# Two more gate pairs as seven half products ahead of attention, and a quota on the filler inside it

## The chip, the cores and the metric

The kernel runs on one core of one Trainium2 chip. The metric is the device time of one execution in microseconds (us). Engines are named as in the profile: PE is the tensor engine's matrix multiply, PEld its weight load, DVE the vector engine, ACT the scalar engine, POOL the general engine, SP the engine that here only issues transfers.

## The reference

One step of a one-layer hybrid encoder, for a prompt of 1024 rows and a sample of 64 rows, all in float32 with 1024 channels:

```python
xn = rms_norm(x, g_pre)
z = xn @ w_in                      # 1024 x 8208
xa, ga, q, k, v, gb, fl, ma, mb = jnp.split(z, np.cumsum(sizes)[:-1], axis=-1)
ua, conv_new = causal_conv(xa, conv_hist, conv_w, conv_b)
ya, h_new = rg_lru(ua, h0, w_rg_a, b_rg_a, w_rg_x, b_rg_x, a_param)
ya = ya * jax.nn.silu(ga)
yb = fox_prompt(q, k, v, logf)     # 16 heads of 64, causal, with forget sums
yb = yb.reshape(B, L, W_B) * jax.nn.silu(gb)
u = jnp.einsum('bsnw,nwd->bsnd', jnp.stack([ya, yb], axis=2), w_branch)
gates = jax.nn.sigmoid(jnp.stack([ma, mb], axis=2))
mix = jnp.sum(gates * u, axis=2) @ w_o
h = x + rms_norm(mix, g_post)      # then a gated per-layer embedding is added
```

`ga`, `gb`, `ma` and `mb` are the four gates: 1024 columns of the input projection each. They need nothing but `xn`, and are wanted only long after attention.

## The kernel before, in words

**Numbers.** A float32 operand is held as a rounded high part and a low part. A product is three matmuls, high by high, high by low and low by high (`three`, L169, whose matmuls carry L170, L171 and L172). The 1088 rows of `xn` (prompt and sample) lie transposed in SBUF.

**Two ways to make 256 columns of the projection.** A *panel* is 128 output columns: for each of three chunks of rows (364, 364, 360) eight steps over the inner dimension, each of three matmuls (`panel_steps`, L189). So a panel is 24 steps or 72 matmuls, and a pair of panels 144. A *quad* makes 256 output columns at once: weights and input are cut into two by two blocks, and seven products of half size stand for eight (`seven`, L860; `product`, L799, whose matmuls carry L805). A quad is seven products of 24 matmuls of 272 rows, so 168 matmuls. It needs sums of weight blocks, made by POOL, ACT and DVE (`split_pair`, L641), and sums of the input blocks, made once.

**The stages in order.** Values (v) for all rows come first (0 to 128 us of the span), then two plain panels (128 to 152), then the quads (152 to 418): eight for k and q, two for some columns of branch A, and `MORE` pairs taken from the end of the list `gates` (L226, L233), here two pairs of `gb`. Results of gates are stored to DRAM. Then comes attention (about 437 to 860 us), then branch A, the two branch projections, the output projection and the tail.

**Attention and its filler.** For each of 16 heads there are four blocks of 256 queries, in the order 0, 3, 1, 2 (`units`, L1242; `q2` is the block's number). A block takes *scores* (matmuls L1125 and L1126; then on DVE the mask and maximum, L1105, on ACT the exponential, L1107, on DVE the reciprocal, L1109, on POOL the scaling, L1110), *turns* (transposes to PSUM, L1147; then ACT copies the high part `th` and DVE the low part `tl`; for the diagonal part the tiles are `diag0h`, `diag0l` and so on) and *values* (four matmuls a turn, L1175 and L1177; then ACT and DVE join the halves in `lo` and `y`). Eight small steps belong to the sample. The gate panels that are left are the *filler*: `filler` (L1038) yields after each step of three matmuls into `acc`. Each panel of filler also brings a weight split (`wh` on ACT, `wl` on DVE, booked by `book_split`, L1021) and three copies out of PSUM (`st` on ACT).

**What sets the order.** PE's order is fixed when the program is built, by a loop (L1333) that keeps a clock `now` of PE and books of ACT, DVE and POOL with costs written in the kernel. A step of scores, turns or values is taken if its inputs have been ready on that clock for `SLACK` = 600 ns. Otherwise a step of filler is taken, if there is one. If there is none, the clock jumps to the moment at which the first step gets ready. ACT, DVE and POOL work in the order of the same books. Before the change 17 panels, 408 steps, are filler.

Of the kernel before, what the change touches and what calls it, by code (L numbers as in the profile page):

```python
# [15 lines left out]
KT = D // P  # L16
# [16 lines left out]
CW = HT // 2  # L33
PLAIN = 2

MORE = 2
W_SC = 1092
GC = 364

# [4 lines left out]
D_W = 1240.0  # L44

AHEAD = 4000
WAKE = 36
GA_EARLY = (1, 3, 5)
LN1P = [1.0 / 15, 1.0 / 13, 1.0 / 11, 1.0 / 9, 1.0 / 7, 1.0 / 5, 1.0 / 3]
# [16 lines left out]
def hybrid_step(tc, a, o):  # L66
# [11 lines left out]
    def f(ap):  # L78
        return ap.bitcast(F32)

    def copy_act(out, in_, scale=1.0):
        return act.activation(out=out, in_=in_, func=AF.Copy, scale=scale)  # L82
# [140 lines left out]
    def cols(c, n=2):  # L223
        return w_in[:, c:c + n * P]

    gates = deque((cols(c + k * P), (d[k], d[k + 1])) for c, d in ((C_MA, d_ma), (C_MB, d_mb), (C_GB, d_gb))  # L226
                  for k in range(0, KT, 2))
# [3 lines left out]
    for (s1, d1), (s2, d2) in (some[:2], some[2:]):  # L231
        quads.append(([s1, s2], (("r", d1), ("r", d2))))
    for _ in range(MORE):  # L233
        src, (d1, d2) = gates.pop()
# [13 lines left out]
    ahead = deque()  # L248
# [8 lines left out]
    def look_ahead():  # L257

        while len(ahead) < 2:
            if held_back[0] and len(gates) <= n_gates - PLAIN // 2:  # L260
                return
            if not (gates or later):
                return
            src, tags = (gates or later)[0]
            if any(not e[3] and max(len(tags), e[4]) > 1 for e in ahead):
                return
            (gates or later).popleft()
            if len(tags) > 1:
                dst = raw_pair
                raws_ = panels(raw_pair)  # L270
            else:
                dst = raw_half[n_single[0] % 2].rearrange("p (k n) -> p k n", k=KT)
                raws_ = [dst]
                n_single[0] += 1
            load_panel(dst, src, tc.keep_in_program_order)
            for tag, raw in zip(tags, raws_):
                ahead.append([tag if isinstance(tag, tuple) else ("r", tag), raw, None, False, len(tags)])
# [26 lines left out]
    def spill(dst, t0, n, z, s=None):  # L304
        s = s or wpool.tile([P, GC], F32, name="st")
        copy_act(s[:, :n], z)
        act.dma_start(dst[:, t0:t0 + n], s[:, :n])
# [141 lines left out]
    g_p = mm.tile([P, 512], F32, name="g_p", tag="acc")  # L449
    for i in range(WAKE):  # L450
        if i == WAKE - 8:
            pe.transpose(g_p[:, :KT], g8[:, :], ident[:KT, :KT])
# [528 lines left out]
    def spent(ns):  # L981
        now[0] += ns

    def book(engine, at, ns, do=None):

        busy = booked[engine]
        while busy and busy[0][1] < now[0] - 20000.0:
            busy.pop(0)
        i = 0
        while i < len(busy) and busy[i][0] < at + ns:  # L990
            at = max(at, busy[i][1])
            i += 1
        busy.insert(i, (at, at + ns))
        if do is not None:
            serial[0] += 1
            heapq.heappush(agenda, (at, serial[0], do))
        return at + ns + HOP

    def catch_up(to=None):
        to = now[0] if to is None else to  # L1000
        while agenda and agenda[0][0] <= to:
            heapq.heappop(agenda)[2]()
# [18 lines left out]
    def book_split():  # L1021

        if ahead and ahead[0][2] is None:
            e = ahead[0]
            raw = e[1]
            wh = wpool.tile([P, KT, P], F32R, name="wh")
            wl = wpool.tile([P, KT, P], F32R, name="wl")
            e[2] = wh, wl

            def low():  # L1030
                sub(dve, wl[:, :, :], raw, f(wh[:, :, :]))
                e[3] = True
                look_ahead()

            at = book("A", now[0] + 5000.0, A_W, lambda: copy_act(wh[:, :, :], raw))
            book("D", at, D_W, low)

    def filler():  # L1038
        left = deque()
        nxt = first_fill  # L1040
        while True:
            if nxt is None:
                look_ahead()
                if not ahead or ahead[0][0][0] != "r":
                    return
                nxt = ahead.popleft()[:3:2]
            (_, dst), w = nxt
            nxt = None
            book_split()

            def evac(c, t0, n, z, dst=dst):
                def do():
                    spill(dst, t0, n, z)
                    left.popleft()

                left.append(book("A", now[0] + 497.0 + HOP_PE, A_ST, do))

            for _ in panel_steps(mm, *w, xs, evac):
                spent(497.0)
                if len(left) > 1:  # L1060
                    catch_up(left[0])
                yield True
# [21 lines left out]
    def load_sample(p):  # L1084
        cols = slice(p * P, (p + 1) * P)
        t = {n: p2.tile(s, F32, name=n, tag=n, bufs=1) for n, s in (("kc", [P, P]), ("vc", [P, P]), ("vn", [DEC, P]))}
        sp.dma_start(t["kc"][:, :], a["cache_k"][:, cols])
        sp.dma_start(t["vc"][:, :], a["cache_v"][:, cols])
        sp.dma_start(t["vn"][:, :], o["v_sample"][:, cols])
        sp.dma_start(f(cs_k[2:, :]), d_cs[2 * p:2 * p + 2].rearrange("h s t -> (h s) t"))  # L1090
        sp.dma_start(f(cs_q[:2, :]).rearrange("s (h t) -> s h t", h=2), d_cq[:, 2 * p:2 * p + 2, :])
        t["ks"] = [p2.tile([P, LS], F32R, name=f"ks{i}", tag=f"ks{i}", bufs=1) for i in "hl"]
        for i in range(2):
            sp.dma_start(f(t["ks"][i][:, PAST:]), d_k[i, p][:, SEQ:])
            for j in range(2):
                js = slice(j * HD, (j + 1) * HD)
                sp.dma_start(f(qs[i][js, js]), d_q[i, p][js, SEQ:])
        smp[p] = t
        smp_at[p] = now[0] + (12000.0 if p else 24000.0)
# [142 lines left out]
    units = [(h, q2) for h in range(NH) for q2 in (0, 3, 1, 2)]  # L1242
    U = len(units)
    UP = 8
    s_q, t_q, v_q = deque(), deque(), deque()
# [46 lines left out]
    def go(step):  # L1292
        kind, x, i = step
        if kind == "s":
            h, q2 = units[x]
            big = q2 >= 2
            tag = "pb" if big else "pm"
            pr = p2.tile([P, 1024 if big else 512], F32, name=tag, tag=tag, bufs=4)
            prs.setdefault(x, []).append(pr)
            s_free["s2" if big else "s1"], due[step] = scores(h, q2, i, pr)  # L1300
            if x == 1 and i == 0:
                load_head(1)
            elif x % 4 == 3 and i == 1:
                load_head(h + 2)
        elif kind == "ss":
            s_free["s1"], due[step] = sample_scores(x)
        elif kind == "v":
            values(x, i, *units[x])
            seen["v"] += 1
            if i == units[x][1] and x % UP in (3, 5) and x // UP + 1 < NP:  # L1310
                load_v(x // UP + 1, x % UP // 4)
        elif kind == "sv":
            sample_values(x)
            if x + 1 < NP:
                load_sample(x + 1)
        else:
            t_free.popleft()
            if kind == "t":
                due[step] = turn(x, i, units[x][1], prs[x])
                seen["t"] += 1  # L1320
            else:
                due[step] = (sample_keys if kind == "sk" else sample_turn)(x)
            t_free.append(due[step])
        done.add(step)
# [4 lines left out]
    load_v(0, 0)  # L1329
    load_v(0, 1, "pb")  # L1330
    load_sample(0)
    fill = filler()
    while s_q or t_q or v_q:  # L1333
        catch_up()
        times = [(i, ready(q[0])) for i, q in enumerate((s_q, t_q, v_q)) if q]
        times = [(i, at) for i, at in times if at is not None]
        best = next((i for i, at in times if at + SLACK <= now[0]), None)
        if best is None:
            if next(fill, False):
                continue  # L1340
            at, best = min((at, i) for i, at in times)
            now[0] = max(now[0], at)
            catch_up()
        go((s_q, t_q, v_q)[best].popleft())
    while next(fill, False):
        catch_up()
    catch_up(float("inf"))
# [266 lines left out]
    fill = panel_steps(mm, *w, xs, lambda c, t0, n, z: spill(d_mb[KT - 1], t0, n, z))  # L1614
# [62 lines left out]
    for of in range(KT):  # L1677
        g = g_next
# [287 lines left out]
    def turn_h(b, pl=None):  # L1966
# [6 lines left out]
        for g in range(3):  # L1973
# [7 lines left out]
            h, l = th[:, k_, :n], (tl[:, k_, :n] if n == P else th[:, k_, DEC:])  # L1981
            with tc.high_priority(AHEAD):
                copy_act(h, t)
# [166 lines left out]
    ss, r = tiny(n, "ss"), tiny(n, "r_r")  # L2150
# [55 lines left out]
```

## Time and profile before

| what | value |
|---|---|
| time, median of three runs | 1464.6 us (1464.26 to 1467.74) |
| the profiled execution's own time | 1467.15 us |
| its span, first to last instruction | 1465.4 us |
| PE busy | 1436.0 us (98%) |
| DVE busy | 893.7 us (61%) |
| ACT busy | 717.1 us (49%) |
| POOL busy | 299.1 us (20%) |
| mean granted clock of PE | 0.994 |

The profiled execution's own time lies 2.55 us above the median, and 1.75 us of its time lie outside its span. PE's matmuls overlap, so a matmul's duration in the profile (0.33 us for 364 rows) is longer than its share of PE's time, and the distance from one start to the next is what counts. A row of the view by windows gives for each engine the busy us and, in brackets, the number of instructions; "acc" are the matmuls of panels, "quad" those of quads.

### The profile page before, as it was taken

What the parts mean: (1) busy time and instruction counts of PE and PEld (TensorE: products, weight loads), DVE (VectorE), ACT (ScalarE), POOL (GpSimd) and SP (SyncE); (2) the same over time, 40 slices, a digit from 0 to 9 for tenths busy, and PEclk for the clock granted to TensorE, in tenths of its full rate; (3) what the DMA queues carried; (4) which work ended last, traced back from release to release, by engine and by line L of the source; (5) the groups of instructions that cost most, each with busy time, mean ns of one, the idle gap of its engine ahead of it and who ended that gap; (6) DMA issues with size and microseconds to landing.
All of it is one profiled execution on the core that took longest, in us unless ns stands there. A gap on an engine that the chain in (4) does not pass through costs nothing.

```text
span 1465.4 us, 25652 instructions
## 1 busy us (share of the span) xinstructions
PE 1436.0 (98%) x9653; PEld 1394.7 (95%) x9653; DVE 893.7 (61%) x1631; ACT 717.1 (49%) x1353; POOL 299.1 (20%) x385
## 2 busy tenths in 40 slices
PE   8999999999999999999999999999999999999997
PEld 8999999999999999999899989999999999879997
DVE  5464866564325666666466555898755574778534
ACT  4423444442215566666456556777444232554633
POOL 0013324323123332333233210221023000000001
PEclk9999999999999999999999999999999999999999
DMA  8457456754276565646545344454278774224111
GB/s 285 143 119 109 130 163 189 181 178 127 78 210 157 120 148 139 141 112 139 118 129 128 61 108 70 86 101 84 99 235 273 257 218 152 100 86 171 43 43 44
DMA packets 149304, 200.64 MB, mean 137 GB/s; under 512 B 24212, under 2 KB 115836, under 8 KB 148156
## 3 DMA queue, kind: packets, MB, share of 16 engines
q1 hardware_dynamic: 129772, 167.06, 44.2%
q10 hardware_dynamic: 17680, 25.64, 5.1%
q0 software_dynamic: 1728, 6.29, 2.3%
q8 instruction: 76, 1.25, 0.4%
q14 instruction: 48, 0.39, 0.1%
HBM read 131.04 MB, written 65.80 MB: 134 GB/s over the span
## 4 chain that ended last, share of the span: by engine, by line
PE 84%; DVE 7%; ACT 4%; DMA 3%; issue 2%; SPq 0%; POOL 0%; ACTq 0%; DVEq 0%; POOLq 0%
PE quad L805 17%; PE acc L170 12%; PE acc L172 12%; PE acc L171 12%; PE q L1853 5%; PE tp L1147 4%; PE pv L1175 2%; PE s L1125 2%; PE s L1126 2%; PE pv L1177 2%; PE vacc L170 1%; PE vacc L171 1%; PE vacc L172 1%; PE vacc L471 1%; PE q L1978 1%
## 5 line engine op out<-in xcount | busy, mean ns | idle before, releaser
L170 PE MATMUL acc<-xh,wh 128*128 128x364 f32 (+1 forms) x768 | 253.2, 330 | 1.3 <-ACT st L82 1.2
L171 PE MATMUL acc<-xl,wh 128*128 128x364 f32 (+1 forms) x768 | 252.0, 328 | 0.0
L172 PE MATMUL acc<-xh,wl 128*128 128x364 f32 (+1 forms) x768 | 251.8, 328 | 0.0
L170 PEld LDWEIGHTS acc<-xh,wh 128*128 128x128 f32 x768 | 144.9, 189 | 2.6 <-ACT st L82 1.9
L171 PEld LDWEIGHTS acc<-xl,wh 128*128 128x128 f32 x768 | 144.7, 188 | 0.5
L172 PEld LDWEIGHTS acc<-xh,wl 128*128 128x128 f32 x768 | 144.5, 188 | 0.0
L1105 DVE CUSTOM_DVE_ANT_0 s<-s,mask 128x1024 f32<-128x1024 f32 (+7 forms) x128 | 95.5, 767 | 26.8 <-PE s L1126 26.7
L85 DVE TENSOR_TENSOR wl<-w_raw,wh 128x1024 fp32r<-128x1024 f32 (+1 forms) x54 | 62.6, 1160 | 67.3 <-ACT wh L82 66.3
L1110 POOL TENSOR_SCALAR pb<-pb,sm 128x896 f32<-128x896 f32 (+1 forms) x64 | 61.8, 966 | 196.2 <-DVE sm L1109 178.2
L82 ACT ACTIVATE wh<-w_raw 128x1024 fp32r<-128x1024 f32 (+1 forms) x66 | 64.3, 976 | 65.6 <-PE quad L805 27.3
L85 DVE TENSOR_TENSOR tl<-tp,th 128x512 fp32r<-128x512 f32 x96 | 65.7, 688 | 35.6 <-ACT th L82 35.6
L805 PE MATMUL quad<-xh,wh 128*128 128x272 f32 x384 | 80.7, 291 | 0.0
L805 PE MATMUL quad<-xl,wh 128*128 128x272 f32 x384 | 79.5, 288 | 0.0
L805 PE MATMUL quad<-xh,wl 128*128 128x272 f32 x384 | 79.4, 288 | 0.0
L82 ACT ACTIVATE th<-tp 128x512 fp32r<-128x512 f32 x96 | 56.9, 596 | 40.6 <-PE tp L1147 33.4
L1107 ACT ACTIVATE pb<-s,nm 128x896 f32<-128x896 f32 (+1 forms) x64 | 61.1, 954 | 30.0 <-DVE nm L1105 27.7
L1125 PE MATMUL s<-k,q 128*128 128x256 f32 (+1 forms) x192 | 67.1, 353 | 0.2 <-ACT pb L1107 0.2
L1147 PE MATMUL tp<-ident,pb 128*128 128x128 f32 x416 | 63.9, 274 | 1.2 <-DVE diag0l L85 0.7
L1126 PE MATMUL s<-k,q 68*128 68x256 f32 (+1 forms) x192 | 65.0, 350 | 0.0
L171 PE MATMUL acc<-ybl,wh 128*128 128x364 f32 (+1 forms) x192 | 62.9, 328 | 0.0
L172 PE MATMUL acc<-ybh,wl 128*128 128x364 f32 (+1 forms) x192 | 62.8, 327 | 0.0
L170 PE MATMUL acc<-ybh,wh 128*128 128x364 f32 (+1 forms) x192 | 62.7, 326 | 0.0
(705 smaller groups left out, 4151.8 us busy)
## 6 DMA issues: line engine op xcount, KB each, us to landing
w_raw<-in_w_in SPq DMA_DIRECT2D x56, 256.0 KB
q<-d_q SPq DMA_DIRECT2D x48, 256.0 KB
k<-d_k SPq DMA_DIRECT2D x48, 256.0 KB
w_raw<-in_w_in SPq DMA_DIRECT2D x64, 128.0 KB
w_raw<-in_w_branch SPq DMA_DIRECT2D x32, 256.0 KB
wl<-w_raw POOLq DMA_DIRECT2D x12, 512.0 KB, 4.6
wraw<-in_w_in SPq DMA_DIRECT2D x20, 256.0 KB
d_k<-oh ACTq DMA_DIRECT2D x16, 272.0 KB
```

What stands on the lines that cost most here:

```text
L82: return act.activation(out=out, in_=in_, func=AF.Copy, scale=scale)
L85: return eng.tensor_tensor(out=out, in0=in0, in1=in1, op=ALU.subtract)
L170: pe.matmul(out, ah, bh, start=start, stop=False)
L171: pe.matmul(out, ah, bl, start=False, stop=False)
L172: pe.matmul(out, al, bh, start=False, stop=stop)
L805: pe.matmul(acc[:, c, :CW], l[:, k, :], r[:, k, c * CW:(c + 1) * CW], start=(first and k == 0 and p == 0), stop=(k == 3 and p == 2), skip_ ...
L1105: at = book("D", now[0] + HOP_PE, per(D_MAX, n), lambda: dve.tensor_tensor_reduce(out=s[:, :n], in0=s[:, :n], in1=m, scale=-1.0, scalar=-N ...
L1110: return free, book("G", at, per(G_NORM, n), lambda: pool.tensor_scalar(out=pr[:, :n], in0=pr[:, :n], scalar1=sm, scalar2=1.0, op0=ALU.mul ...
L1125: pe.matmul(s[:, c0:c0 + w], t["q1"][:, q0:q0 + P], t["k1"][:, c0:c0 + w], start=True, stop=False)
L1126: pe.matmul(s[:, c0:c0 + w], t["q2"][:HD + 4, q0:q0 + P], t["k2"][:HD + 4, c0:c0 + w], start=False, stop=True)
L1147: pe.transpose(tp[:, o0 + i * P:o0 + (i + 1) * P], pr[par][:, kb * P:(kb + 1) * P], ident[:, :])
L1853: pe.matmul(acc, l[:, k, :], r[:, k, :], start=(first and k == 0 and i == 0), stop=(k == 3 and i == 2), skip_group_check=not first)
```

## The change

`MORE` becomes 4: the pairs of `gb` columns 0 to 3 of eight leave the filler and become two more quads, so there are 14 quads and 13 panels, 312 steps, of filler. And the loop no longer takes filler whenever nothing else is ready. The first `HEAD` = 72 steps (three panels) are free; after that the number of steps taken may not run ahead of the share of attention's own PE work that is done, weighed by columns (`own_time`). If the quota is used up, the clock jumps to the next step's moment, as it did before when no filler was left.

```diff
-MORE = 2
+MORE = 4
...
+HEAD = 72
...
+    def own_time(step):
+
+        kind, x, i = step
+        if kind == "s":
+            full = 256 * (units[x][1] + 1)
+            return sum(2 * (0.44 * min(512, full - c0) + 8) for c0 in range(0, full, 512))
+        if kind == "t":
+            return 109.0 * (3 if i == units[x][1] else 4)
+        return {"v": 480.0, "sk": 109.0, "ss": 440.0, "st": 218.0, "sv": 840.0}[kind]
+
     fill = filler()
+    own_total = sum(own_time(step) for q in (s_q, t_q, v_q) for step in q)
+    own = 0.0
+    filled = 0
+    n_fill = 3 * KT * (1 + sum(e[0][0] == "r" for e in ahead) + sum(len(g[1]) for g in gates))
     while s_q or t_q or v_q:
...
         if best is None:
-            if next(fill, False):
+            if filled < HEAD + (n_fill - HEAD) * own / own_total and next(fill, False):
+                filled += 1
                 continue
             at, best = min((at, i) for i, at in times)
             now[0] = max(now[0], at)
             catch_up()
-        go((s_q, t_q, v_q)[best].popleft())
+        step = (s_q, t_q, v_q)[best].popleft()
+        own += own_time(step)
+        go(step)
```

The order on PE is the same up to the early heads and differs after them. The first place is in head 10, between the turn of its block 0 (three transposes into `tp`) and the values of that turn (`pv<-diag1l`). In both orders four values matmuls of another block and the first matmul of the sample's scores (`s<-ksh,qsh`) follow the turn; the rows below begin behind these. This is PE before:

```order
L170 MATMUL s_8620<-ksh,qsh 128x192
L171 MATMUL s_8620<-ksl,qsh 128x192
L172 MATMUL s_8620<-ksh,qsl 128x192
L1209 MATMUL s_8620<-cs_k,cs_q 128x192
L1147 MATMUL tp_8630<-ident,pb 128x128 x4
L170 MATMUL acc<-xh_110,wh 128x360
L171 MATMUL acc<-xl_112,wh 128x360
L172 MATMUL acc<-xh_110,wl 128x360
L170 MATMUL acc<-xh_110,wh 128x360
L171 MATMUL acc<-xl_112,wh 128x360
L172 MATMUL acc<-xh_110,wl 128x360
L1147 MATMUL tp_8650<-ident,pb 128x128 x4
```

The values `pv<-diag1l` stand in the row behind. The same place on PE with the change (lines are one higher):

```order
L171 MATMUL s_8832<-ksh,qsh 128x192
L172 MATMUL s_8832<-ksl,qsh 128x192
L173 MATMUL s_8832<-ksh,qsl 128x192
L1210 MATMUL s_8832<-cs_k,cs_q 128x192
L171 MATMUL acc<-xh_109,wh 128x364
L172 MATMUL acc<-xl_111,wh 128x364
L173 MATMUL acc<-xh_109,wl 128x364
L1176 MATMUL pv<-diag1l,vv 128x256
```

One step of filler and two turns of the next block have gone from between the turn and its values. The second place is the last block of the last head, where before no filler is left. PE before, three turns and the values of earlier ones:

```order
L1147 MATMUL tp_10525<-ident,pb 128x128 x4
L1175 MATMUL pv<-tl,vv 128x256
L1177 MATMUL pv<-th,vv 128x256
L1175 MATMUL pv<-tl,vv 128x256
L1177 MATMUL pv<-th,vv 128x256
L1147 MATMUL tp_10539<-ident,pb 128x128 x4
L1175 MATMUL pv<-diag2l,vv 128x256
L1177 MATMUL pv<-diag2h,vv 128x256
L1175 MATMUL pv<-diag2l,vv 128x256
L1177 MATMUL pv<-diag2h,vv 128x256
L1147 MATMUL tp_10554<-ident,pb 128x128 x3
```

The same turns with the change:

```order
L1148 MATMUL tp_10594<-ident,pb 128x128 x4
L1176 MATMUL pv<-tl,vv 128x256
L1178 MATMUL pv<-th,vv 128x256
L1176 MATMUL pv<-tl,vv 128x256
L1178 MATMUL pv<-th,vv 128x256
L171 MATMUL acc<-xh_110,wh 128x360
L172 MATMUL acc<-xl_112,wh 128x360
L173 MATMUL acc<-xh_110,wl 128x360
L1148 MATMUL tp_10612<-ident,pb 128x128 x4
L1176 MATMUL pv<-diag2l,vv 128x256
L1178 MATMUL pv<-diag2h,vv 128x256
```

A step of filler now stands between each turn and the next to the end of attention.

## The prediction, made before the changed kernel ran

> **What bounds the kernel now.** I read the page first, then the windows of the stages that the change touches, then PE's waits in attention, then single places in time. The page:
>
> ```profile
> span 1465.4 us, 25652 instructions
> PE 1436.0 (98%) x9653; PEld 1394.7 (95%) x9653; DVE 893.7 (61%) x1631; ACT 717.1 (49%) x1353; POOL 299.1 (20%) x385
> ...
> PE 84%; DVE 7%; ACT 4%; DMA 3%; issue 2%; SPq 0%; POOL 0%; ACTq 0%; DVEq 0%; POOLq 0%
> ```
>
> PE is busy for 98% of the span and is 84% of the chain that ended last: the kernel is bound by PE, and only what makes PE's work less, or makes PE wait, moves the time. By windows: the two plain panels, a stretch of quads that write gates, attention while filler lasts, its end without filler, and a stretch with a dip.
>
> ```profile
> 128.00:152.00 24.00, 23.91 (x145) 23.60 (x144) 18.95 (x16) 11.76 (x17) 11.40 (x8) 1.00 0.58 91
> 340.00:400.00 60.00, 60.00 (x480) 60.00 (x479) 24.33 (x33) 15.08 (x24) 11.82 (x8) 1.00 0.27 76
> 437.00:843.00 406.00, 402.32 (x2714) 387.08 (x2713) 250.86 (x649) 238.81 (x561) 132.08 (x198) 1.00 0.57 127
> 843.00:860.00 17.00, 13.61 (x95) 11.42 (x94) 10.52 (x24) 11.07 (x25) 3.92 (x8) 1.00 0.61 123
> 700.00:750.00 50.00, 46.50 (x303) 44.39 (x302) 28.30 (x74) 26.63 (x64) 15.10 (x23) 0.97 0.52 118
> ```
>
> The columns are length, then busy us and count for PE, PEld, DVE, ACT and POOL, then the granted clock. With filler PE lacks 406 - 402.32 = 3.7 us in 406; without it, 17 - 13.61 = 3.4 us in 17. Together 7.1 us. DVE (62%) and ACT (59%) are well filled in attention, but neither is its bound. The waits of PE in attention name what they were:
>
> ```profile
> PE pv L1175 <- DVE y L1186: 3.9, 2, 3.3
> PE tp L1147 <- DVE tl L85: 1.2, 2, 0.8
> PE pv L1175 <- ACT lo L82: 0.9, 3, 0.5
> PE tp L1147 <- DVE diag0l L85: 0.7, 1, 0.7
> PE s L1125 <- ACT pb L1107: 0.2, 1, 0.2
> ```
>
> Nearly all of the first stretch's loss is one wait of 3.3 us. So the filler covers attention's hand-overs between engines almost completely, and where it ends they show at once.
>
> **The work on PE: two pairs.** Removed from attention are four panels, two pairs. The first window holds exactly one pair: 144 matmuls in 23.9 us, 0.166 us each. The second holds quads alone: 480 matmuls in 60.0 us, 0.125 us each, so a quad of 168 costs 21.0 us. Each pair gets 23.9 - 21.0 = 2.9 us cheaper, two 5.8 us. What else a pair brings lies beside PE. In those 60 us of quads, about three pairs, DVE worked 24, ACT 15 and POOL 12 us, splits and block sums included, and PE did not pause; the transfers took 0.27 of the DMA engines, against 0.57 in attention, so the pairs' weights (SP) and results (ACT's and SP's queues) find more room there than where they come from. I cost these at nothing; without that cover the whole 5.8 us could go.
>
> From attention the panels also take work of the helpers:
>
> ```profile
> L82 ACT ACTIVATE st<-acc 128x364 f32<-128x364 f32 (+1 forms) x51 | 24.1, 472 | 52.4 <-PE acc L172 44.7 <-DMA d_ma<-st 7.2
> L85 DVE TENSOR_TENSOR wl<-w_raw,wh 128x1024 fp32r<-128x1024 f32 x16 | 20.2, 1261 | 20.0 <-ACT wh L82 20.0
> L82 ACT ACTIVATE wh<-w_raw 128x1024 fp32r<-128x1024 f32 x19 | 20.0, 1054 | 1.5 <-PE acc L171 1.0 <-DMA q<-d_q 0.5
> ```
>
> Twelve copies of 0.47 and four splits of 1.05 are 9.9 us of ACT, four of 1.26 are 5.0 us of DVE. Neither is on the path, so this pays nothing by itself; it leaves ACT at about 240 and DVE at about 256 us of a stage that shrinks from 423 to some 375: 64 and 68%.
>
> **The cover in attention.** This is the open term. Filler in the first stretch of attention and in the end:
>
> ```profile
> 437.00:843.00 406.00, 211.86 (x1115) 182.82 (x1113) 0.00 (x0) 21.72 (x46) 1.00 0.57 127
> 843.00:860.00 17.00, 0.74 (x5) 0.86 (x6) 0.00 (x0) 0.45 (x1) 1.00 0.61 123
> ```
>
> 1115 matmuls of 0.166 us are 185 us, 46% of the 406; in the end 5 are 5%. With the change 312 steps are left; some 38 run before the first scores, as now. So 274 steps, 822 matmuls, 136 us fall into about 375 us: 36%. Loss rises from almost nothing (0.4 us beside the one wait) at 46% to 3.4 of 17 = 20% at 5%. The straight line puts 36% at 10/41 of the way: 4.9%, 18 us. If the cover has room to spare, the curve lies below it; a square puts it at 1.2%, 4 us. Whether there is room is seen at single turns. One without a queue in front, with two values matmuls of earlier turns, the transposes, the high part and the low part (start, duration):
>
> ```profile
> 544.06 0.28 PE L1177 MATMUL pv<-th,vv 128*128 128x256 f32 x1
> 544.18 0.28 PE L1175 MATMUL pv<-tl,vv 128*128 128x256 f32 x1
> ...
> 544.42 0.60 PE L1147 MATMUL tp<-ident,pb 128*128 128x128 f32 x4
> 545.05 0.60 ACT L82 ACTIVATE th<-tp 128x512 fp32r<-128x512 f32 x1 [1.25 <-PE tp L1147]
> 545.68 0.69 DVE L85 TENSOR_TENSOR tl<-tp,th 128x512 fp32r<-128x512 f32 x1
> ```
>
> Values matmuls start 0.12 us apart. Four transposes take PE 0.44 us (0.11 each: eight last 1.03 in the next rows, four 0.60), to 544.86; the low part is there at 546.37, 1.5 us later. And two turns behind a weight split of the filler:
>
> ```profile
> 578.59 1.03 PE L1147 MATMUL tp<-ident,pb 128*128 128x128 f32 x8
> 580.68 1.05 ACT L82 ACTIVATE wh<-w_raw 128x1024 fp32r<-128x1024 f32 x1
> 581.75 1.09 ACT L82 ACTIVATE th<-tp 128x512 fp32r<-128x512 f32 x2
> 582.30 1.40 DVE L85 TENSOR_TENSOR wl<-w_raw,wh 128x1024 fp32r<-128x1024 f32 x1
> 583.63 1.27 DVE L85 TENSOR_TENSOR tl<-tp,th 128x512 fp32r<-128x512 f32 x2
> ```
>
> Eight transposes end at 579.47, the low parts at 584.90: 5.4 us, and PE did not wait, because it had filler. The place in head 10 now has between turn and values: eight values and sample matmuls (0.12 each at most), two turns (0.88) and six filler matmuls (1.0), so 2.8 us; with the change eight (0.96) and three (0.5), 1.5 us. That holds for the first kind of turn with nothing to spare and fails for the second. So there will be waits, but short ones, where a queue stands in front. I take 10 us, between 4 and 18; the outer bounds are 2 us (all turns like the first) and about 28 us (a loss for each split, below). The end gains from the quota: its short waits are
>
> ```profile
> 846.93 0.66 PE L1147 MATMUL tp<-ident,pb 128*128 128x128 f32 x4 [0.66 <-DVE diag0l L85]
> 851.95 0.63 PE L1147 MATMUL tp<-ident,pm 128*128 128x128 f32 x4 [0.76 <-DVE tl L85]
> 858.20 0.38 PE L1175 MATMUL pv<-tl,vv 128*128 128x256 f32 x1 [0.57 <-DVE y L1186]
> ```
>
> and a step of filler, 0.5 us, now stands between such turns. This is contained in the 10 us, since they stand for all of attention.
>
> **The slow clock.** After its one long wait PE ran slowly:
>
> ```profile
> 709.56 0.60 PE L1147 MATMUL tp<-ident,pb 128*128 128x128 f32 x4
> 713.48 0.38 PE L1175 MATMUL pv<-tl,vv 128*128 128x256 f32 x1 [3.32 <-DVE y L1186]
> 716.59 0.51 PE L171 MATMUL acc<-xl,wh 128*128 128x364 f32 x1
> 716.89 0.51 PE L172 MATMUL acc<-xh,wl 128*128 128x364 f32 x1
> ```
>
> Starts are 0.30 us apart instead of 0.166, and the window 700 to 750 has a clock of 0.97, so 0.03 x 50 = 1.5 us were lost beside the wait. The waits at the end, up to 0.76 us, left the clock at 1.00. I expect short waits and count the 1.5 us as gone; if a long one returns, it stays. [...]
>
> **The sum.** Work -5.8; waits 10 instead of 7.1, +2.9; clock -1.5: -4.4 us. On the profiled execution that is 1467.15 - 4.4 = 1462.75; it lies 2.55 us above the median of the three runs, and from the median the forecast is 1464.6 - 4.4 = 1460.2 us. With W for the waits, the time is 1464.6 - 14.4 + W. About 0.3%, 4.4 us, is what a measurement of this kernel can tell from no change, so "faster" is W under 10.0 and "slower" W over 18.8.
>
> **Rivals.** *The cover has room (W about 2).* For it: of the waits of before only one was long, and turns of the first kind need 1.5 us, which the order leaves even at the short place. Against: ACT and DVE get fuller. Time 1464.6 - 12.4 = 1452.2 us; chance 0.15.
>
> *The turn's queue decides, and the kernel gets slower.* Place: a turn behind a weight split, about 11 times in attention for the 13 panels. It took 5.4 us, and where the order leaves 2.9 us or less, PE waits 2.5 us: 28 us for all. It decides above 1.7 us for each, when W passes 18.8. For it: no filler can be drawn there once the quota is used. Against: the books of ACT and DVE place a split where they see a gap. At 2.0 us each W is 22 and the time 1472.2 us; chance 0.16.
>
> *The clock falls.* If waits as long as 3.3 us come at a third of the splits, four of them, each adds 1.5 us; with W at 20 that gives -14.4 + 20 + 6 = +11.6, 1476.2 us. Only one wait in 423 us was of that kind; chance 0.04. [...]
>
> *The change does not do what it says.* The two new quads run no faster than panels because splits or stores come late: +5.8 on the forecast, 1466.0 us. The window 340 to 400, without a pause of PE, speaks against it; chance 0.05.
>
> **Chances.** The forecast, W from 4 to 18, has 0.60; a little over half of that, 0.33, is under W = 10.0. Faster: 0.33 + 0.15 = 0.48. Same: 0.27 + 0.05 = 0.32. Slower: 0.16 + 0.04 = 0.20. The range, 1452 to 1472 us, reaches from the first rival to the second and leaves out the clock's case and the outer part of the second.
>
> **What would show it.** Right: quads in a window of 14 x about 22 us that ends some 42 us later, still 0.125 us a matmul; attention about 45 us shorter; waits of PE there of about 10 us in total, most of them on `tl`, `diag` low parts or `lo`, single ones under 2 us; no clock under 1.00 between 480 and 880 us. Wrong: waits over 19 us or under 4 us in that stretch, pauses inside the two new quads, or a change of more than 2 us in the stages behind attention, which the change leaves alone.

## The result, and the profile after

The changed kernel takes 1475.07 us (median of six runs, 1473.38 to 1477.11), the kernel before 1467.08 us (six runs, 1464.26 to 1468.12). The ratio is 1.0052, with a 95% interval from 1.0041 to 1.0062: slower by about half a per cent, 7.6 us. The forecast was a ratio of 0.997, and the time lies above the upper end of the range. The kernel before takes 2.5 us more by its six runs than by the three from which the forecast started, so times are best compared as ratios. In what follows "+x us" is always the ratio to the kernel before on the same chip, applied to 1467 us.

The page of the changed kernel:

```profile
span 1471.7 us, 25813 instructions
PE 1433.2 (97%) x9701; PEld 1387.1 (94%) x9701; DVE 907.5 (62%) x1649; ACT 720.3 (49%) x1353; POOL 305.9 (21%) x393
...
PE 75%; DVE 9%; DMA 6%; ACT 5%; issue 3%; POOL 1%; SPq 1%; ACTq 0%; DVEq 0%; POOLq 0%
```

PE has 2.8 us less to do than before, and the span is 6.3 us longer. The chain that ended last tells it at once: PE's share of it fell from 84 to 75%, and DMA's rose from 3 to 6%, DVE's from 7 to 9%. By stages, from first start to first start on PE:

| stage | before | after | difference |
|---|---|---|---|
| first quad to last quad | 266.4 us | 308.6 us | +42.2 |
| last quad to first scores | 19.0 us | 19.0 us | 0 |
| attention, first scores to last values | 421.6 us | 384.6 us | -37.1 |
| from there to PE's last matmul | 598.2 us | 599.2 us | +1.0 |

Four panels, 288 matmuls of 0.1657 us on average, are 47.7 us of work that left attention; with +42.2 the work gained 5.5 us. But attention got only 37.1 us shorter, so 10.6 us were lost there. The windows of the changed kernel (length, then busy us and count of PE, PEld, DVE, ACT and POOL, granted clock, DMA share, GB/s): quads, all of attention, and three stretches of it.

```profile
152.40:461.20 308.80, 307.11 (x2455) 305.97 (x2454) 172.37 (x246) 110.97 (x198) 95.12 (x81) 1.00 0.54 148
480.00:864.60 384.60, 372.49 (x2512) 350.42 (x2510) 255.39 (x667) 240.36 (x566) 132.87 (x201) 0.99 0.55 124
540.00:600.00 60.00, 56.06 (x375) 52.94 (x374) 36.31 (x97) 34.46 (x82) 20.28 (x31) 0.97 0.62 119
750.00:800.00 50.00, 47.93 (x321) 45.06 (x320) 34.19 (x88) 30.92 (x73) 16.52 (x25) 0.97 0.53 120
800.00:850.00 50.00, 47.83 (x326) 44.79 (x325) 34.07 (x94) 32.15 (x76) 18.27 (x27) 1.00 0.46 86
```

Attention's PE stands idle for 384.6 - 372.5 = 12.1 us, where 7.1 us were idle before, and the clock falls twice (0.97 in two of the stretches), where it fell once. That explains some 6.5 of the 10.6 us. The rest is hidden in the busy figure: a filler matmul is drawn 0.33 us long but follows the one ahead of it after 0.166 us, so a wait under 0.16 us leaves no gap. PEld, the weight load, shows it: 34.2 us idle after, against 24.5 us (421.9 - 397.4) in attention before. From before to after PE's idle time grew by 5.0 us and PEld's by 9.7 us, where the loss is 10.6 us: here PEld's idle time is the better measure.

PE's waits from 440 to 880 us of the changed kernel (us in total, times, longest):

```profile
PE s L1126 <- ACT pb L1108: 3.6, 1, 3.6
PE tp L1148 <- DVE tl L86: 2.9, 2, 1.8
PE tp L1148 <- POOL pb L1111: 1.7, 1, 1.7
PE tp L1148 <- POOL pm L1111: 1.4, 4, 0.7
PE pv L1176 <- DVE y L1187: 1.2, 3, 0.6
```

Four single waits, at 561, 625, 778 and 809 us, make up 8.2 us, and the first (3.59 us) is a little longer than the one of before (3.32 us). The longest, by what SP issues and what ACT does (starts and us; SPq and ACTq are issues of transfers):

```profile
547.65 2.59 SPq L255 DMA_DIRECT2D w_raw<-in_w_in  x4
550.35 2.27 SPq L1163 DMA_DIRECT2D d_y<-y  x1
...
554.96 0.47 ACT L83 ACTIVATE st<-acc 128x364 f32<-128x364 f32 x1 [0.41 <-PE acc L173]
559.63 0.33 ACTq L308 DMA_DIRECT2D d_ma<-st  x1
560.00 0.38 ACT L83 ACTIVATE lo<-pv 64x256 f32<-64x256 f32 x1 [4.57 <-DMA w_raw<-in_w_in]
560.41 0.90 ACT L1108 ACTIVATE pb<-s,nm 128x768 f32<-128x768 f32 x1
561.45 0.50 PE L1126 MATMUL s<-k,q 128*128 128x512 f32 x1 [3.59 <-ACT pb L1108]
```

ACT finished a filler copy at 555.43 and then stood for 4.2 us ahead of an instruction that only sends that copy to DRAM. It went on when a load of filler weights, `w_raw`, had landed. The exponential `pb`, which the copy has nothing to do with, stood behind it, and PE behind that. The other waits are relatives. Here is the chain that ended last up to the wait at 778 us (start, us, what):

```profile
761.79 7.28 DMA q<-d_q
769.14 5.48 DMA v_raw<-out_v_prompt
774.67 0.41 POOL vv L1078
...
777.02 1.11 POOL pb L1111
778.18 0.90 PE tp L1148 x3
```

POOL had the split of the next head's values (from 774.67 us) ahead of the scaling of `pb` (777.02), and these values came late: their load was issued at 769.14 us, 0.07 us after another had landed (761.79 + 7.28 = 769.07), and took 5.48 us. At 809 us (and so at 625) the join `y` wanted a buffer whose store had not landed, 8.1 us after its issue and right behind a load of weights, and a turn's low part `tl` stood behind the join:

```profile
808.01 0.42 DVE L1187 TENSOR_TENSOR y<-pv,lo 64x256 f32<-64x256 f32 x1 [2.26 <-DMA d_y<-y]
...
809.08 0.66 PE L1148 MATMUL tp<-ident,pb 128*128 128x128 f32 x4 [1.82 <-DVE tl L86]
```

The one long wait of the kernel before was of the same kind. In its chain the landing of a load of `v_raw` released ACT's issue of a store, and 2 us later PE's wait of 3.3 us ended (713.48 us); between them ACT copied `th`, and DVE made `tl` and `y`:

```profile
708.63 2.70 DMA v_raw<-out_v_prompt
711.41 0.33 ACTq L307
711.78 0.61 ACT th L82
```

### The profile page after: what moved, and what is told of

It is laid out like the page before. It is cut to its first block, busy times and chain, and to the rows that moved or that the text cites. A ratio compares the mean times of both kernels' runs of the same rounds, so it can differ in the third digit from the quotient of the medians.

```text
span 1471.7 us, 25813 instructions
## 1 busy us (share of the span) xinstructions
PE 1433.2 (97%) x9701; PEld 1387.1 (94%) x9701; DVE 907.5 (62%) x1649; ACT 720.3 (49%) x1353; POOL 305.9 (21%) x393
## 4 chain that ended last, share of the span: by engine, by line
PE 75%; DVE 9%; DMA 6%; ACT 5%; issue 3%; POOL 1%; SPq 1%; ACTq 0%; DVEq 0%; POOLq 0%
PE quad L806 20%; PE acc L171 9%; PE acc L173 9%; PE acc L172 9%; PE q L1871 5%; PE tp L1148 3%; PE pv L1176 2%; PE pv L1178 2%; PE s L1126 2%; PE s L1127 2%; PE vacc L171 1%; PE vacc L172 1%; PE vacc L173 1%; DMA d_y<-y 1%; DMA w_raw<-in_w_in 1%
## 5 line engine op out<-in xcount | busy, mean ns | idle before, releaser
L171 PE MATMUL acc<-xh,wh 128*128 128x364 f32 (+1 forms) x672 | 225.4, 335 | 3.2 <-ACT st L83 3.2
L173 PE MATMUL acc<-xh,wl 128*128 128x364 f32 (+1 forms) x672 | 220.4, 328 | 0.0
L172 PE MATMUL acc<-xl,wh 128*128 128x364 f32 (+1 forms) x672 | 220.3, 328 | 0.0
L171 PEld LDWEIGHTS acc<-xh,wh 128*128 128x128 f32 x672 | 126.7, 189 | 6.4 <-ACT st L83 4.0
L172 PEld LDWEIGHTS acc<-xl,wh 128*128 128x128 f32 x672 | 126.7, 189 | 0.7
L173 PEld LDWEIGHTS acc<-xh,wl 128*128 128x128 f32 x672 | 126.3, 188 | 0.0
L806 PE MATMUL quad<-xh,wh 128*128 128x272 f32 x448 | 93.9, 291 | 0.0
L806 PEld LDWEIGHTS quad<-xh,wh 128*128 128x128 f32 x448 | 70.4, 188 | 0.2
L806 PEld LDWEIGHTS quad<-xh,wl 128*128 128x128 f32 x448 | 70.6, 188 | 0.0
L806 PEld LDWEIGHTS quad<-xl,wh 128*128 128x128 f32 x448 | 70.5, 188 | 0.0
```

Of the source, the lines that this page charges most:

```text
L171: pe.matmul(out, ah, bh, start=start, stop=False)
L172: pe.matmul(out, ah, bl, start=False, stop=False)
L173: pe.matmul(out, al, bh, start=False, stop=stop)
L806: pe.matmul(acc[:, c, :CW], l[:, k, :], r[:, k, c * CW:(c + 1) * CW], start=(first and k == 0 and p == 0), stop=(k == 3 and p == 2), skip_ ...
```

## The experiments

Three theories. A: the loss comes from transfers that land late behind the loads of filler weights and stop an engine, with all that stands behind on it. B: it is the thin cover itself, many small waits because fewer filler steps stand between work and what needs it. C: the quota costs. Each edit below is against the changed kernel. All medians, with their ratios to the kernel before:

| run | median, us | ratio | 95% interval | attention, us |
|---|---|---|---|---|
| changed kernel | 1475.07 | 1.0052 | 1.0041 to 1.0062 | 384.6 |
| no_loads | 1465.46 | 0.9983 | 0.9972 to 0.9994 | 374.0 |
| quota_only | 1462.18 | 0.9957 | 0.9945 to 0.9969 | 415.1 |
| quads_only | 1480.36 | 1.0080 | 1.0068 to 1.0093 | 392.8 |
| y_now | 1474.93 | 1.0040 | 1.0025 to 1.0054 | 382.8 |
| v_later | 1474.73 | 1.0046 | 1.0031 to 1.0061 | 385.8 |
| store_sp | 1479.43 | 1.0078 | 1.0063 to 1.0093 | 375.6 |
| all_three | 1475.61 | 1.0054 | 1.0034 to 1.0075 | 370.9 |
| no_loads_two | 1459.56 | 0.9942 | 0.9927 to 0.9957 | 412.0 |
| late_store | 1466.03 | 0.9997 | 0.9987 to 1.0006 | 376.7 |
| late_four | 1460.71 | 0.9947 | 0.9929 to 0.9965 | 371.7 |
| late_two | 1458.29 | 0.9933 | 0.9916 to 0.9950 | 411.2 |
| quota_none | 1470.27 | 1.0017 | 1.0005 to 1.0030 | 428.7 |
| loads_two | 1470.27 | 1.0018 | 1.0008 to 1.0028 | 378.9 |
| loads_one | 1480.28 | 1.0083 | 1.0066 to 1.0099 | 391.4 |

**no_loads: the filler's weights aren't loaded.**

```diff
-            load_panel(dst, src, tc.keep_in_program_order)
+            if isinstance(tags[0], tuple) or not skipping[0]:
+                load_panel(dst, src, tc.keep_in_program_order)
```

`skipping[0]` is set when attention begins.

> The changed kernel, but from the start of attention the filler's weight loads are left out (its panels are multiplied with what lies in the buffer; the gates that they give are not the reference's). Splits, copies, stores and PE's work stay. Theory A (landings): the loss in attention comes from a few long waits, 1.1 to 3.6 us each, that end with the landing of a transfer queued behind a burst of weight loads (store of y, load of v, store of a filler chunk), and from the slow clock after two of them. Then without the loads these waits go and the time falls by 7 to 11 us against the changed kernel, to 1464 to 1468 us. Theory B (thin cover): the filler is too thin for the hand-overs between engines, the waits are spread, and the loads have nothing to do with it. Then the time falls by 0 to 2 us, 1473 to 1475 us.

All of attention in this run:

```profile
481.20:855.30 374.10, 369.27 (x2511) 347.76 (x2510) 255.18 (x667) 240.08 (x566) 132.93 (x201) 1.00 0.49 115
```

The work of the engines is that of the changed kernel, attention is 10.5 us shorter, and the clock stays at 1.00. No wait is left above 1.0 us. Against the changed kernel this is -10 us: theory A has most of the loss.

**quota_only: the quota without the two quads.**

```diff
-MORE = 4
+MORE = 2
```

> The kernel before with the quota alone: two gate pairs as quads, 17 panels of filler, spread to the end of attention. PE's work is that of before. Both theories: the end of attention, where before had 3.4 us of waits in 17, is covered, and in the middle 33 to 38 steps a tenth of attention stand where 34 to 43 stood: 2 to 5 us faster than before, 1462 to 1465 us. A third theory C: the quota itself costs, because a step taken at the end of the quota has no slack of 600 ns: then it is slower than before by 3 us or more.

```profile
437.70:853.00 415.30, 412.49 (x2800) 395.58 (x2798) 260.96 (x671) 248.70 (x581) 134.69 (x201) 1.00 0.56 125
```

-6.3 us with the work of before: PE's idle time in attention goes from 7.1 to 2.8 us and the slow clock from it. Theory C falls; the quota is the part of the change that pays.

**quads_only: the two quads without the quota.**

```diff
-            if filled < HEAD + (n_fill - HEAD) * own / own_total and next(fill, False):
-                filled += 1
+            if next(fill, False):
```

> The two more quads without the quota: filler is taken greedily and ends after 7 of 10 parts of attention's own work; the last 3 parts, about 65 us of PE work, have none, and no weight loads either. Theory B (thin cover): in those the waits are 20% of the time as at the end of attention before, about 16 us, where the quota has about 8: 5 to 10 us slower than the changed kernel, 1480 to 1485 us. Theory A (landings): without bursts of loads the last parts wait little, and the time is that of the changed kernel or up to 4 us less, 1471 to 1475 us.

+11.7 us, 4 us more than the changed kernel: theory B's side, a little under its 5 to 10 us. The filler ends after 7/10 of attention's own work, and from there PE waits in short pieces. Two of them:

```profile
858.34 0.39 PE L1176 MATMUL pv<-diag2l,vv 128*128 128x256 f32 x1 [1.04 <-DVE diag2l L86]
...
864.14 0.66 PE L1148 MATMUL tp<-ident,pb 128*128 128x128 f32 x4 [0.90 <-DVE tl L86]
```

So both theories have something: without cover the hand-overs cost, and with thin cover the late transfers do.

**y_now, v_later, store_sp: one late transfer at a time.** The store of `y` is sent at once, the values of a head are split 6 us later by the books, the filler's stores are issued by SP instead of ACT.

```diff
-            leave(1)
+            leave(0)
```

```diff
-            at = now[0] + 8000.0 + 3000.0 * j
+            at = now[0] + 14000.0 + 3000.0 * j
```

```diff
-                    spill(dst, t0, n, z)
+                    spill(dst, t0, n, z, by=sp)
```

> The changed kernel, but each block's store of y is issued when it is ready instead of one block later (two of the four long waits of the changed kernel, 1.1 and 1.8 us, ended with the landing of such a store). Theory A (landings): those two waits go, 2 to 4 us less than the changed kernel, 1471 to 1473 us. Theory B (thin cover): no difference beyond 1 us.

> The changed kernel, but POOL's split of v is booked 6 us later, so that the scaling of the scores does not stand behind a load of v that is late. Of the two longest waits of the changed kernel (3.6 us at 561 us, 1.7 us at 778 us, each with 3.4 us of slow clock after it) the second should go, with its clock. Theory A (landings): 3 to 4 us less than the changed kernel, 1471 to 1472 us. Theory B (thin cover): within 1 us of the changed kernel, 1474 to 1476 us.

> The changed kernel, but the stores of the filler's chunks are issued by SP and not by ACT. At 555 us ACT stood 4.2 us before such an issue, and the wait of PE at 561 us was behind it. Theory A (landings): this wait and its slow clock go, 4 to 6 us less than the changed kernel, 1469 to 1471 us; if SP's own loads then stand behind the stores, half of it comes back. Theory B (thin cover): within 1 us of the changed kernel.

None came to the time that theory A gave, though each took away its own wait. Without the waits at 625 and 809, y_now kept 3.9 us at 561 and 2.0 us at 778, and the slow clock behind each. v_later lost the wait at 778, but the one at 561 grew to 5.2 us:

```profile
PE s L1126 <- ACT pb L1108: 5.2, 1, 5.2
PE tp L1148 <- DVE tl L86: 2.9, 2, 1.9
```

store_sp has no wait at 561 and an attention 9 us shorter, and pays for it ahead of attention, which begins 13 us later after the last quad: its first stores stand on SP behind the loads of the first head, and PE waits for their buffer.

```profile
PE acc L171 <- ACT st L83: 12.0, 2, 11.1
```

**all_three and no_loads_two.** all_three joins the three edits; no_loads_two is no_loads with `MORE = 2`.

> The changed kernel with y stored at once, v split later and the filler's stores on SP: all that stood behind a late landing is taken away, the loads stay. Theory A (landings): the time comes down to that of the kernel without loads, 1464 to 1468 us, with no clock under 1.00 in attention. Theory B (thin cover): not under 1472 us.

> The quota with two quads as before (17 panels of filler) and, from the start of attention, no weight loads for the filler (the gates of these panels are not the reference's). Against the same with four quads and no loads, 1465.5 us, it has 5.8 us more work on PE and 37 instead of 24 steps of filler in a tenth of attention. If the thin cover alone, without landings, costs as much as the two quads give, this is equal to it or faster: 1460 to 1465 us (Theory B's share). If only the landings matter, it is slower by up to 5.8 us: 1469 to 1471 us (Theory A alone).

all_three came to +7.9 us, which by the sentence above would be theory B. But it lost 10.7 us in the same wait for a store's buffer ahead of attention, and in attention it has no long wait and no slow clock: 370.9 us against 384.6. no_loads_two is 6.0 us faster than no_loads, though it has 5.8 us more work on PE. With no loads in either, the two quads lose some 12 us beside their gain in work: theory B is right too, beside A. Not all of the 12 us is cover in attention: in the profiled executions the part behind the last values is 4 us longer in no_loads than in no_loads_two (610.9 and 606.9 us).

**late_store, late_four, late_two.** The stores go by SP only after attention's seventh step. late_store is the changed kernel with that alone, late_four has the other two edits as well, late_two is late_four with `MORE = 2`.

```diff
-                    spill(dst, t0, n, z)
+                    spill(dst, t0, n, z, by=sp if len(done) > 7 else act)
```

> The changed kernel with y stored at once, v split later, and the filler's stores on SP from the first scores' steps on; ahead of them on ACT, since on SP they stood behind the first head's loads and held PE for 13 us. Theory A (landings): attention as in the run with all three, some 14 us shorter than in the changed kernel, or 10 if the order comes out less well: 1462 to 1466 us. Theory B (thin cover alone): 1472 us or more.

> The same three edits with two quads of gate pairs and the quota (17 panels of filler). Without loads this order gave 1459.6 us, with them 1462.2 us. Theory A (landings): the difference of 2.6 us is landings, and most of it goes: 1459 to 1461 us. If filler as dense as this covers late landings anyway: 1462 us. In both cases it should be faster than before and than the changed kernel, and faster than the same edits with four quads by 2 to 5 us, which is Theory B's share.

> Of the three edits the last one alone: the changed kernel with the filler's stores on SP from the first scores' steps on, y and v as in the changed kernel. Theory A (landings): the wait of 3.6 us at 561 us and its slow clock (1.7 us) go, and the waits on y (1.3 and 2.0 us) and on v (1.9 us, with 1.7 us of slow clock) stay: 1468 to 1471 us, between the changed kernel (1475.1) and the one with all three (1460.7). If it gives all of the 14 us, stores of the filler on ACT were the whole cause; if it gives under 3 us, the three only work together.

late_store is 8 us faster than the changed kernel by one engine's name on some stores, more than the 4 to 7 us expected; its trace keeps a wait of 2.0 us on `y` and a slow clock at 770 us. late_four is 15 us faster, below the times expected, and now 7.8 us faster than the kernel before. late_two is faster still, 2.4 us by the medians on the same chip, and is the fastest of all these kernels. Attention in late_four, then in late_two:

```profile
482.30:854.10 371.80, 368.06 (x2512) 347.91 (x2510) 256.19 (x667) 238.73 (x566) 132.77 (x201) 1.00 0.57 128
```

```profile
438.30:849.70 411.40, 411.23 (x2800) 395.44 (x2798) 261.13 (x671) 246.98 (x581) 133.08 (x201) 1.00 0.56 126
```

With two quads PE is idle for 0.2 us of attention, with four for 3.7, and PEld for 16.0 and 23.9 us. So even with no long wait left, two quads more lose 7.9 us of PEld's time and save 5.8 us of work.

**quota_none: no gate quads at all** (`MORE = 0`).

> The quota with no gate pair as a quad ahead of attention: ten quads, 21 panels of filler. PE has 5.8 us more work than with two, and some 49 steps of filler in a tenth of attention instead of 37. Theory A alone: no long wait was left with two, so the time is 1462.2 + 5.8 = 1468 us. Theory B (cover): if more filler still covers small waits, part of the 5.8 us comes back: 1464 to 1467 us.

It came out above both theories. A wait of 3.8 us with slow clock stood at 669 us, with the chain of the long wait of before: a load of `v_raw` lands, ACT's store goes out, `th`, `tl` and `y` follow. And the quota did not place all filler: what was left took 55 us behind attention, where the changed kernel needs 17. So it decides nothing about the cover, but shows that a late transfer can return in another order.

**loads_two, loads_one: why ACT stands.** By then it was open whether ACT stands because the transfers are backed up as such, or because its issue waits for one older transfer. The author's guess was the second, by a counter of landed transfers that the store and the weight load have in common ("the counters" in the two expectations). No trace shows such a counter; what a trace shows is when ACT went on, and which landing came just ahead. The edit lets a pair of filler panels load in two transfers, or in one, instead of four:

```diff
-        n = KT // 4
-        for i in range(4):
+        n = KT // parts[0]
+        for i in range(parts[0]):
```

`parts[0]` is 4 up to attention, then 2 or 1, and 4 again behind it. Bytes and the order of the engines stay; the number of transfers changes. The author expected ACT to stand at that store again with one transfer, and not with two.

> In attention each filler pair's weights come in two transfers of 512 KB instead of four of 256 KB: same bytes, same order on the engines. [...] If the counters are what stops ACT: the wait at 561 and its slow clock are gone, the waits on y and on v stay roughly, 1468 to 1471 us. If the transfers are late only because so many bytes are under way, nothing that ACT sees changes: the wait at 561 stays at 3 to 5 us, 1473 to 1477 us.

> As the run with two transfers, but each pair's weights in one transfer of 1 MB. [...] If the counters are what stops ACT: the wait near 561 stays, at 3.6 us or more, and the time is 1473 to 1478 us, so one transfer is slower than two. If fewer transfers help by themselves (issues on SP, cost per transfer), one is at least as good as two, and both the same way; if bytes under way decide, both are like the changed kernel.

The same place, ACT's store, with two transfers:

```profile
554.51 0.47 ACT L83 ACTIVATE st<-acc 128x364 f32<-128x364 f32 x1 [0.41 <-PE acc L173]
555.01 0.35 ACTq L312 DMA_DIRECT2D d_ma<-st  x1
555.46 0.38 ACT L83 ACTIVATE lo<-pv 64x256 f32<-64x256 f32 x1 [0.48 <-PE pv L1183]
```

And with one:

```profile
556.51 0.47 ACT L83 ACTIVATE st<-acc 128x364 f32<-128x364 f32 x1 [0.41 <-PE acc L173]
564.95 0.33 ACTq L312 DMA_DIRECT2D d_ma<-st  x1
565.32 0.38 ACT L83 ACTIVATE lo<-pv 64x256 f32<-64x256 f32 x1 [8.34 <-DMA w_raw<-in_w_in]
```

With two the store goes out at once, with one ACT stands for 8.0 us and PE for 7.4. The medians of the whole kernels differ by 10.0 us, two at +2.6 and one at +12.2 us (over the 1473 to 1478 us expected), where the changed kernel with four is at +7.6. The bytes are the same in all three, and the time does not go with the number of transfers; it goes with how long ACT stood at this store until a load of weights had landed: 4.2 us with four, 0.03 us with two, 8.0 us with one. That is shown for the wait at 561; why the store waits for that landing is not shown. That v_raw's load at 769.14 went out 0.07 us after `q<-d_q` had landed looks like the same, but rests on one place of the trace. The late store of `y`, 8.1 us from issue to landing right behind a load of weights, is another case; that the load slows it is likely, since without the loads no wait over 1.0 us is left, but was not tried by itself.

## Why the prediction failed, point by point

**The work: right.** -5.8 us was forecast, -5.5 us measured. A quad takes 21.1 us, and there is no pause inside the new ones: PE was busy for 307.1 of 308.8 us, and the 1.7 us that it lacks were lacking before too (265.0 of 266.7). What a pair brings beside PE was rightly costed at nothing there.

**The filler's share: right.** 36% of attention was forecast; in the changed kernel it is 824 matmuls of 0.166 us, 137 of 384.6 us, 36%:

```profile
480.00:864.60 384.60, 173.53 (x824) 133.92 (x822) 0.00 (x0) 16.13 (x34) 0.99 0.55 124
```

**The cover: the failed step.** "So there will be waits, but short ones, where a queue stands in front. I take 10 us, between 4 and 18". By the measure that it used, PE's idle time, 12.1 us came, within its bounds; but that measure misses the short waits between matmuls, so "waits 10 instead of 7.1, +2.9" stood where the loss was some 9 us without the clock. With the hidden waits that makes about 16 us, still between 4 and 18, but 6 us over the 10 of the sum. And not all waits were short: four of them reach 1.1 to 3.6 us. The step looked at single turns, at ACT's and DVE's queues and at splits. No row of it asked what a transfer that is late does to an engine and to the work that stands behind on it. The one long wait of before was the sample of that, and was told as a single case; its chain, followed further back, shows a load that released ACT's store. In the terms of the forecast's sum: work -5.5 for -5.8, waits +8.9 for +2.9, clock +1.7 for -1.5, and +1.0 behind attention, which it put at nothing. That is +6.1 us in place of -4.4, and the two profiled spans differ by 6.3 us.

**The clock: wrong.** "I expect short waits and count the 1.5 us as gone; if a long one returns, it stays." A slow clock came twice, at 563 and 778 us, so +1.7 us or so in place of -1.5.

**The quota: mis-sized on the other side.** The prediction put its gain inside the 10 us, with at most the 3.4 us of the uncovered end in view. By itself it gives 6.3 us. Without it the change would have cost 11.7 us.

**The rivals.** The second, slower with 1472.2 us, has the sign and even the size (+7.6 us on its base, as measured), but by luck, since it does not have the mechanism: none of the four long waits stands behind a weight split; two are ACT and POOL held up until other transfers had landed (for ACT loads_two and loads_one show it too, for POOL the chain alone), two are DVE waiting for a store to land. No run here took the splits away by themselves, so what they add to the small waits stays open. "The clock falls" was seen twice, not four times. That the cover has room is refuted, and that the quads run no faster too.

**What was to show it.** Of the signs that it named for being right, those on the quads held and those on attention failed: it is 37 us shorter instead of about 45, one wait, on `pb`, is over 2 us, and the clock fell under 1.00. Of the three signs for being wrong none came: PE's idle time, 12.1 us, lies between 4 and 19, there is no new pause in the quads, and behind attention nothing moved by over 2 us. So by its own signs the case lay between right and wrong.

The sum by the runs, in steps of ratio: the quota -6.3; the two further quads without any long wait, late_four against late_two, +2.0 (work -5.8, cover +7.8); and the late transfers, whose removal brings -15.4 with four quads and -3.5 with two, +11.9. Together +7.6 us. This closes by construction, since the steps are differences between the same runs, and the split between the last two is not exact. Attention, of the profiled executions in the table, tells it a second way. 47.7 us of filler left it. It got 30.5 us shorter from quota_only to the changed kernel, 38.0 from no_loads_two to no_loads, and 39.5 from late_two to late_four. So 17.2 us are lost with all late transfers, 9.7 and 8.2 without most of them: cover is 8 to 10 us, late transfers 7 to 9. And the late transfers' part belongs to this order. A change of the program's order or of its transfers can move these waits: loads_two, with other transfers, lost the longest, and quota_none, in another order, has one of 3.8 us.

## What to carry to other kernels

Filler is also a reserve that hides late transfers: the same three edits brought 3.5 us with 17 panels of filler and 15.4 with 13. Before some of it is moved away, look in the trace for engines that stand ahead of an issue or of a load, for these waits can surface. An issue of a transfer on an engine that computes can stand until another transfer has landed (ACT for 4.2 us in the changed kernel, for 8.0 in loads_one), and everything behind it stands too. Here it paid to put it on an engine that only issues (late_store, 8 us; not where it stands behind that engine's own loads, as in store_sp), or to load in another number of transfers (loads_two, 5.0 us). Cost a loss of cover by PE's starts or by the weight loads' idle time, not by the idle time of overlapping matmuls: of the loss of 10.6 us PEld's idle time showed 9.7 us here, PE's 5.0.

## What the runs showed of the hardware that was not expected

The slow clock does not need a wait of 3.3 us, as in the kernel before. In the changed kernel it came right after 1.72 us at 778 and not after 1.82 us at 809; matmuls of filler are 0.30 us apart behind the first:

```profile
778.18 0.90 PE L1148 MATMUL tp<-ident,pb 128*128 128x128 f32 x3 [1.72 <-POOL pb L1111]
```

In quads_only many waits of about 1 us followed each other with the clock at 1.00. So in these traces the length of one gap doesn't decide by itself.

No run was made to test what else does. In the changed kernel the clock was 0.50 for 3.41 us from 563.02 us and for 3.41 us from 778.06 us; the two points are 215.04 us apart, 63 times 3.41 us. The 3.41 us ahead of the second, the slow ones, and 3.41 us at the same spacing, nine lengths on, with most of the wait at 809 are:

```profile
774.65:778.06 3.41, 1.46 (x8) 0.94 (x8) 1.79 (x6) 1.75 (x5) 3.22 (x5) 1.00 0.44 127
778.06:781.47 3.41, 3.29 (x11) 3.10 (x12) 1.32 (x3) 0.69 (x2) 0.46 (x2) 0.50 0.24 54
805.37:808.78 3.41, 1.89 (x12) 1.59 (x10) 0.94 (x3) 1.65 (x5) 2.33 (x4) 1.00 0.42 143
```

The wait at 778 falls nearly whole into the first row, beside a gap of 0.34 us, and PE is idle for 1.95 of 3.41 us; the wait at 809 is cut at 808.78, PE is idle for 1.52 us of the third row, and the clock stayed at 1.00. Ahead of the slow clock at 563 PE was idle for 1.84 of 3.41 us (559.61 to 563.02), and in the kernel before, ahead of the one at 714.24 us, for 2.65 (710.83 to 714.24). But 1.80 us of idle time from 1075.02 to 1078.43 us in the changed kernel left the clock at 1.00. That it is the idle time over some microseconds that counts, and not one gap, is the author's estimate from these few places; no run varied it.
